# Input projections of two quarters at a time through DRAM, with S5 in batches of two groups beside them

## The chip, the core and the metric

One core of a Trainium2 chip runs the kernel. Its engines have instruction queues of their own: TensorE (PE) multiplies matrices, VectorE (DVE), ScalarE (ACT) and GpSimd (POOL) work on tiles, and SyncE (SP) issues transfers. What counts is the device time of one execution in microseconds; the median of several runs is compared.

## What is computed

One layer of a decoder is applied to 2048 new tokens of one sequence and, with stored states, to one further token of each of 8 samples. The width is 1024. Two mixers run on the same projections: S5, a diagonal state space with 32 groups of 64 complex states, and a gated delta net of 4 heads of 128 channels in chunks. Their outputs are joined and projected, and a feed-forward part with a short causal convolution follows:

```
def layer(x, ...):
    n = rmsnorm(x, norm1_g)
    proj = n @ w_in                                   # 512 of S5 | q, k, v | z | beta, a
    y_s5, s5_re, s5_im = s5_mixer(u_s5, ...)          # scan over time, gelu, gate w_glu
    y_gdn, gdn_s, gdn_buf = gdn_mixer(qkv, z, ...)    # conv of 4, silu, delta rule in chunks, norm, gate z
    x = x + jnp.concatenate([y_s5, y_gdn], axis=-1) @ w_out
    y_ffn, ffn_buf = conv_ffn(rmsnorm(x, norm2_g), ffn_buf, ffn_w_up, ffn_conv_w, ffn_w_down)
    return x + y_ffn, ...
```

All values are fp32. The outputs are the tokens, normed once more, and the mixers' and convolutions' last states.

## The kernel before

The tokens are cut into four quarters of 512 (`QT`); quarter 0 carries the 8 samples behind its tokens (520 columns). Activations lie transposed, channels on partitions. A product in fp32 is made of three products of float32r parts: every operand is split into a high part (`hi`, a copy on ACT) and an exact rest (`lo`, a subtraction on DVE; some on POOL), and `mm3` (lines 286 to 289) adds hi x hi, hi x lo and lo x hi. A projection of 128 output channels (`proj`, `mm24`) is thus 24 matmuls: 8 k tiles by three lines, L287 to L289. Its weights are loaded by `wcols` (L303) into a tile `wr` and split by `wsplit` through `split` (L71 on ACT, L72 on DVE or POOL). Each quarter of each use splits its weights anew; the eight tiles `W` and two tiles `wr` are rings that all of them share.

The stages, in the order of emission:

- Norm 1 of the quarters 3, 2, 1, 0 (`norm_first`), the S5 tables (`s5_setup`, to DRAM), and the S5 input projection of all quarters (`s5_in`, four weight tiles kept), whose result `u` goes to DRAM with time as (position in a chunk of 8, chunk).
- S5 proper: eight batches of four groups over all tokens (`s5_batch`), mixed with the heads of quarter 0 by the string `MIXERS`. A batch's first part (`b`) has the input product (L636), a rotation (L638 to L642) and 64-step scans in chains over four quarters (L649); its second part (`h`) has the rotation back (L656, L657), three output products (L665 to L668) and a gelu, and stores `y` to DRAM. Two of the wide multiplies (L641, L656) are POOL's.
- A head of a quarter has three parts: `F`, `gdn_front` (four projections for k, q, v, z from the quarter's normed tokens `nT`, the short convolution L820 to L824, norms, decay products), `I`, `gdn_inverse` (a triangular inverse by 31 steps L906, L907 and merges), `B`, `gdn_back` (the chunk recurrence, L953 to L966, output norm, gate, a store to `mixT` in DRAM).
- The output gate of S5 (`s5_glu`), and per quarter the output projection with residual (`ffn_out`, L1144), norm 2, the FFN's 22 steps of two channel tiles with up and down products (`ffn`, `ffn_down`, L1097), the final norm.

The string `FFN` puts the heads of quarters 1 to 3 beside the FFN of the quarter before: `r` is the next piece of the gate, output projection or FFN, `N` norms the next quarter again from stored x (`norm_again`, L276 to L283) and makes its columns (`gdn_cols`), `S` is the samples' delta step (`gdn_sample`), `G` stores final states. A scheduler then orders each engine's instructions from emission order, priorities and estimated times; engines execute their queue in that order, and a tile's ring of buffers decides when the next load may start.

## Time and profile before

| what | value |
|---|---|
| median of 3 runs | 2872.86 us (2869.67 to 2876.55) |
| span of the profiled execution, its own time here | 2874.3 us |
| PE busy | 2715.0 us, 94% |
| DVE busy | 2176.9 us, 76% |
| ACT busy | 1476.0 us, 51% |
| POOL busy | 609.6 us, 21% |
| DMA | 329.30 MB, mean 115 GB/s |
| mean granted TensorE clock | 0.964 of full speed |

The span runs from the first to the last instruction of one profiled execution. Busy shares are averages over stages that have different limits; the windows further down cut the span at the stages' ends. [...] Matmuls overlap in their records, so that a matmul's own duration is longer than the distance to the next one's start.

### The profile page before, as it was taken

The page shows a single profiled execution, that of the slowest core. Times are in us where ns is not written, and L with a number is a line of the kernel's source. Part 1 is how long each engine was busy: PE and PEld are TensorE (multiplying, and loading weights), DVE is VectorE, ACT ScalarE, POOL GpSimd, SP SyncE. Part 2 cuts the span into 40 slices and gives each one's busy share as a digit, 9 for nine tenths or more (in the row PEclk, how much of TensorE's full clock was granted, in tenths as well). Part 3 has the DMA queues.
Part 4 walks back from the last instruction along what each step waited for, and adds up shares of the span by engine and source line. Part 5 has one row for each costly group of instructions (what it writes and reads, how often), then busy time and mean ns, then how long its engine had stood idle before and what let it go on. Part 6 is the DMA issues. An engine that isn't in the chain of part 4 may idle for free.

```text
span 2874.3 us, 45554 instructions
## 1 busy us (share of the span) xinstructions
PE 2715.0 (94%) x16103; PEld 2337.9 (81%) x16103; DVE 2176.9 (76%) x4964; ACT 1476.0 (51%) x3051; POOL 609.6 (21%) x970
## 2 busy tenths in 40 slices
PE   6998788899999999998899999999999998999998
PEld 4798676786888999998887888878888787888887
DVE  8949898856688787778588687887768667676666
ACT  4446565653665554455564554555545445444444
POOL 4325332100121122222221100113211112211112
PEclk9999887898999999999999999999999999999999
DMA  7644433453644232233533333245333334523332
GB/s 205 199 134 132 113 109 92 105 133 104 182 110 117 77 103 87 89 97 111 155 115 109 100 91 98 84 137 174 93 96 97 90 93 144 157 88 96 95 97 74
DMA packets 457657, 329.30 MB, mean 115 GB/s; under 512 B 74960, under 2 KB 412249, under 8 KB 457412
## 3 DMA queue, kind: packets, MB, share of 16 engines
q1 hardware_dynamic: 447091, 297.77, 35.8%
q0 software_dynamic: 10336, 28.61, 3.4%
q8 instruction: 127, 2.08, 0.3%
q14 instruction: 103, 0.84, 0.1%
HBM read 279.29 MB, written 47.29 MB: 114 GB/s over the span
## 4 chain that ended last, share of the span: by engine, by line
PE 66%; DVE 17%; DMA 8%; ACT 4%; issue 3%; POOL 0%; SPq 0%; DVEq 0%; POOLq 0%; ACTq 0%
PE psmm L287 15%; PE psmm L288 15%; PE psmm L289 15%; PE psd L287 5%; PE psd L288 5%; PE psd L289 5%; DVE wlo L72 3%; DVE t L823 1%; ACT whi L71 1%; DVE X L907 1%; DMA xr<-xTD 1%; DMA mr<-mixT 1%; DVE x L1097 1%; DVE hh L649 1%; DMA wr<-in_w_out_dram 1%
## 5 line engine op out<-in xcount | busy, mean ns | idle before, releaser
L287 PE MATMUL psmm<-nT,whi 128*128 128x512 f32 (+2 forms) x3232 | 1115.5, 347 | 45.2 <-ACT whi L71 9.6
L288 PE MATMUL psmm<-nT,whi 128*128 128x512 f32 (+2 forms) x3232 | 1110.3, 344 | 4.8 <-DVE nT L224 3.0
L289 PE MATMUL psmm<-nT,wlo 128*128 128x512 f32 (+2 forms) x3232 | 1107.2, 343 | 1.7 <-POOL wlo L72 1.0
L287 PEld LDWEIGHTS psmm<-nT,whi 128*128 128x128 f32 x3232 | 622.5, 193 | 120.3 <-ACT whi L71 11.7
L288 PEld LDWEIGHTS psmm<-nT,whi 128*128 128x128 f32 x3232 | 624.5, 193 | 73.1 <-DVE nT L224 4.5
L71 ACT ACTIVATE whi<-wr 128x1024 fp32r<-128x1024 f32 x404 | 427.2, 1059 | 496.3 <-PE psmm L288 309.9
L289 PEld LDWEIGHTS psmm<-nT,wlo 128*128 128x128 f32 x3232 | 623.0, 193 | 72.4 <-issue 1.9
L72 DVE TENSOR_TENSOR wlo<-wr,whi 128x1024 fp32r<-128x1024 f32 x388 | 482.3, 1246 | 193.2 <-ACT whi L71 187.4
L1097 DVE TENSOR_TENSOR x<-psd,x 128x512 f32<-128x512 f32 (+2 forms) x464 | 255.6, 558 | 127.3 <-PE psd L289 125.2
L287 PE MATMUL psd<-gt,whi 128*128 128x512 f32 (+2 forms) x928 | 323.6, 350 | 12.7 <-DVE x L1097 10.4
L288 PE MATMUL psd<-gt,whi 128*128 128x512 f32 (+2 forms) x928 | 316.5, 342 | 0.0
L289 PE MATMUL psd<-gt,wlo 128*128 128x512 f32 (+2 forms) x928 | 314.6, 340 | 0.0
L1254 DVE SCALAR_TENSOR_TENSOR t<-raw,cc,t 128x512 f32<-128x512 f32 x352 | 271.5, 772 | 37.1 <-ACT t L1251 27.5
L1255 POOL COPY halo<-raw 128x2 f32<-128x2 f32 x176 | 49.6, 282 | 850.7 <-DVE raw L1250 765.9
L1251 ACT ACTIVATE t<-raw,cc 128x512 f32<-128x512 f32 (+1 forms) x176 | 127.2, 723 | 170.0 <-DVE raw L1250 156.7
L287 PEld LDWEIGHTS psd<-gt,whi 128*128 128x128 f32 x928 | 175.0, 189 | 42.5 <-DVE x L1097 18.8
L72 POOL TENSOR_TENSOR gt<-s,gt 128x512 fp32r<-128x512 f32 (+1 forms) x88 | 134.7, 1531 | 350.4 <-ACT gt L71 341.6
L288 PEld LDWEIGHTS psd<-gt,whi 128*128 128x128 f32 x928 | 175.1, 189 | 20.6
L289 PEld LDWEIGHTS psd<-gt,wlo 128*128 128x128 f32 x928 | 174.9, 189 | 20.8
L1107 POOL TENSOR_TENSOR sq<-sq 128x256 f32<-128x256 f32 (+1 forms) x112 | 109.8, 981 | 219.1 <-ACT sq L1105 213.1
L906 DVE TENSOR_TENSOR tm<-X,N 128x124 f32<-128x124 f32 (+30 forms) x496 | 125.4, 253 | 26.7 <-DMA N<-nD 17.6
L907 DVE TENSOR_TENSOR X<-X,tm 128x124 f32<-128x124 f32 (+30 forms) x496 | 129.6, 261 | 8.4
(503 smaller groups left out, 3666.5 us busy)
## 6 DMA issues: line engine op xcount, KB each, us to landing
wr<-in_ffn_w_up_dram SPq DMA_DIRECT2D x176, 512.0 KB
wr<-in_ffn_w_down_dram SPq DMA_DIRECT2D x88, 512.0 KB
wr<-in_w_in_dram SPq DMA_DIRECT2D x64, 512.0 KB
wr<-in_w_out_dram SPq DMA_DIRECT2D x64, 512.0 KB
xTD<-xT SPq DMA_DIRECT2D x32, 256.0 KB
N<-nD SPq DMA_DIRECT2D x16, 512.0 KB
mr<-mixT SPq DMA_DIRECT2D x32, 256.0 KB
xr<-xTD SPq DMA_DIRECT2D x32, 256.0 KB
```

Source lines behind the costliest of these rows:

```text
L71: nc.scalar.activation(hi, raw, AF.Copy)
L72: (eng or nc.vector).tensor_tensor(lo, raw, f32(hi), op=OP.subtract)
L287: nc.tensor.matmul(out, lhsT=wh, rhs=xh, start=first, stop=False)
L288: nc.tensor.matmul(out, lhsT=wh, rhs=xl, start=False, stop=False)
L289: nc.tensor.matmul(out, lhsT=wl, rhs=xh, start=False, stop=last)
L906: nc.vector.tensor_tensor(m, X[:, :, j:j + 1].to_broadcast(sh), N[:, j:j + 1, j + 1:].to_broadcast(sh), op=OP.mult)
L907: nc.vector.tensor_tensor(X[:, :, j + 1:], X[:, :, j + 1:], m, op=OP.add)
L1097: nc.vector.tensor_tensor(x2[:, j, b0:b1], p, x2[:, j, b0:b1], op=OP.add)
L1107: c.nc.gpsimd.tensor_tensor(acc[0], acc[0], s, op=OP.add)
L1251: nc.scalar.activation(t[:, :n], raw[:, 2:2 + n], AF.Copy, scale=w[2])
L1254: nc.vector.scalar_tensor_tensor(t[:, :QT], raw[:, j:j + QT], w[j], t[:, :QT], op0=OP.mult, op1=OP.add)
L1255: nc.gpsimd.tensor_copy(c.halo[:, ch], raw[:, QT:QT + 2])
```

## The change

All input projections leave the heads. A generator `in_pass` takes two quarters: it loads and splits the four S5 weight tiles and makes `u` of both quarters; then, four column tiles of one head at a time (k, q, v, z), it projects both quarters with one load and split of the weights, evicts PSUM to a tile `rw` (ACT, or DVE with the row scales in quarter 1), and stores it to `rawD` in DRAM. It runs first for quarters 1 and 0 (string `PASS1`, with three heads' parts of quarter 0), then for 3 and 2 (string `PASS2`, with S5's batches, the columns, the samples' step and the last head of quarter 0). S5's rest is in `MIXERS` behind it, then come the FFN's pieces: nine for the gate and quarter 0's output projection without a head, then three lines of sixteen pieces with four heads each, then quarter 3's FFN. `gdn_front` loads q, k, v (with three halo columns) and z of its quarter from `rawD` through SP instead of projecting them. S5 runs in 16 batches of two groups; its two multiplies on POOL go to DVE. All lo parts of weights are DVE's now (16 of 404 were POOL's), and there are 376 instead of 404. `norm_again` falls away, and the S5 rotation tables are made in two passes of 16 groups, not four of 8.

```diff
-UNQ = (3, 2, 1)
+UNQ = (1,)
-WQ = lambda nc: nc.gpsimd
+WP = 3000
-PRE = "uuuuucuulu"
-MIXERS = "bFIbhbFhhbIbBhbhFBbFIhhbBhx"
-FFN = "IBNFrrIrFrrrrSrrBFrIIBrrrFIrBBrNFrIFrrrrBIrrFrrBIrrrrBFrrrrINBrFIrFrrBFIrrrrIrBrBrrrrrrrFrrrrrIBrrrGrrrrrrrrrrrrrrrrrrrr"
+PASS1 = "ppppppppFppppppppIFppppppppBIFpppppppp32BI"
+PASS2 = "cFSbBbIphBpbphppbphppbphppbphppbphppbphppbphpppbphpppbphppbphppb"
+MIXERS = "hbhbhbhhhhhhhhx"
+FFN = ("rrrrrrrrr"
+       "rrFrrIrBFrrIrBFrrIrBFrrIrBrr"
...
+       "G")
...
+def in_pass(c, qs, nTs, rsBs):
...
+    ws = [wcols(c, c.w_in, t * 128) for t in range(4)]
+    for q in qs:
+        for t in range(4):
+            s5_in(q, t, ws[t])
+    yield
+    for h in range(4):
+        ts = [t + h for t in (4, 0, 8, 12)]
+        with c.tc.high_priority(WP):
+            ws = [wcols(c, c.w_in, 512 + ti * 128) for ti in ts]
+        for q in qs:
+            for ti, w in zip(ts, ws):
+                n = ncols(q)
+                raw = c.V("rw")
+                for b0, b1, p in projw(c, q, nTs[q], w):
+                    evict(raw[:, b0:b1], q, p, b0, b1)
+                nc.sync.dma_start(c.rawD[ti, :, q * QT:(q + 1) * QT], raw[:, :QT])
...
+                yield
...
-    """4 groups (64 channels) over all prompt tokens, and their samples"""
-    gs = slice(4 * t, 4 * t + 4)
+    gs = slice(2 * t, 2 * t + 2)
...
-    nc.gpsimd.tensor_tensor(Xw[:, :, :, 0:64], Xw[:, :, :, 0:64], St[:, :, None, 1:65].to_broadcast(sh(64)), op=OP.mult)
+    tt(Xw, Xw, St[:, :, None, 1:65].to_broadcast(sh), op=OP.mult)
...
-    nc.gpsimd.tensor_tensor(hw, H, St[:, :, None, 0:64].to_broadcast(sh(64)), op=OP.mult)
+    tt(hw, H, St[:, :, None, 0:64].to_broadcast(sh), op=OP.mult)
...
-def gdn_front(c, q, h, nT, col, hp):
+def gdn_front(c, q, h, col, hp):
...
+    def load(dst, ti):
+        if q:
+            nc.sync.dma_start(dst[:, 0:QT + 3], c.rawD[ti, :, q * QT - 3:(q + 1) * QT])
...
-        pr = proj(c, q, nT, c.w_in, 512 + ti * 128)
...
-        for b0, b1, p in pr:
-            nc.scalar.activation(raw[:, 3 + b0:3 + b1], p, AF.Copy)
-            nc.scalar.activation(t[:, b0:b1], p, AF.Copy, scale=w[3])
+        load(raw, ti)
+        nc.scalar.activation(t[:, :n], raw[:, 3:3 + n], AF.Copy, scale=w[3])
```

What stands in the engines' queues now, at three places. First PE in the S5 stage. `pss` are S5's products, `psmm` projections, `psi` and `psb` pieces of a head. Before:

```order
L636 MATMUL pss<-U,Fm 128x256 x2
L928 MATMUL psi<-T2T_145,Z 32x32 x4
L636 MATMUL pss<-U,Fm 128x256 x2
L289 MATMUL psmm<-nT,wlo 128x264
L938 MATMUL psi<-TT,LT 64x64 x4
L636 MATMUL pss<-U,Fm 128x256 x2
L941 MATMUL psi<-T2T_145,Z_2865 64x64 x4
L636 MATMUL pss<-U,Fm 128x256 x2
L959 MATMUL psb<-rv,T2T_145 128x128
L665 MATMUL pss<-U,Tm 128x256
L963 MATMUL psb<-vn,kg 128x128
L964 MATMUL psb<-vn,AT 128x128
```

After, in the second pass:

```order
L274 MATMUL psmm<-nT,whi 128x512
L275 MATMUL psmm<-nT,whi 128x512
L276 MATMUL psmm<-nT,wlo 128x512
L274 MATMUL psmm<-nT,whi 128x512
L275 MATMUL psmm<-nT,whi 128x512
L276 MATMUL psmm<-nT,wlo 128x512
L674 MATMUL pss<-U,Tm 128x256
L685 MATMUL pss<-Us,Fm 128x8 x2
L689 MATMUL pss<-Us,Tm 16x8
L690 MATMUL pss<-h_4674,Em 16x8
L676 MATMUL pss<-hh,Em 128x256
L677 MATMUL pss<-hw,Es 128x256
```

The S5 products and head pieces that followed one another with single projection matmuls between them now stand behind whole projections over 512 columns (L274 to L276 are L287 to L289 of before).

Second, PE in the new order where the second pass ends:

```order
L276 MATMUL psmm<-nT,wlo 128x512
L674 MATMUL pss<-U,Tm 128x256
L685 MATMUL pss<-Us,Fm 128x8 x2
L689 MATMUL pss<-Us,Tm 16x8
L690 MATMUL pss<-h_4674,Em 16x8
L689 MATMUL pss<-Us,Tm 16x8
L676 MATMUL pss<-hh,Em 128x256
L677 MATMUL pss<-hw,Es 128x256
L674 MATMUL pss<-U,Tm 128x256
L676 MATMUL pss<-hh,Em 128x256
L677 MATMUL pss<-hw,Es 128x256
L690 MATMUL pss<-h_4674,Em 16x8
```

Up to there projections alternate with S5; from there on only S5's small products stand in the queue, until the gate's first products. Before, no such place exists, since projections of heads run on through the FFN.

Third, DVE where quarter 0's FFN hands over to quarter 1's output projection (`x` from `psmm` and `xr` is the residual sum that evicts a product, `wlo` a split, L823 and L841 the convolution of a head's front). Before:

```order
L195 SCALAR_TENSOR_TENSOR nrm<-x_6015,cc,rq 128x256
L72 TENSOR_TENSOR wlo<-wr,whi 128x1024
L72 TENSOR_TENSOR nT_6016<-nrm,nT_6016 128x256
L1144 TENSOR_TENSOR x_6015<-psmm,xr 128x256 x2
L957 SCALAR_TENSOR_TENSOR rv<-psb,col,vt 128x128
L195 SCALAR_TENSOR_TENSOR nrm<-x_6015,cc,rq 128x256 x2
L72 TENSOR_TENSOR wlo<-wr,whi 128x1024
L72 TENSOR_TENSOR nT_6016<-nrm,nT_6016 128x256 x2
L961 TENSOR_SCALAR vn<-psb,hc 128x128
L72 TENSOR_TENSOR wlo<-wr,whi 128x1024
L823 SCALAR_TENSOR_TENSOR t<-raw,cc,t 128x512 x3
```

After:

```order
L1163 TENSOR_TENSOR x_7807<-psmm,xr 128x256 x3
L71 TENSOR_TENSOR wlo<-wr,whi 128x1024
L1163 TENSOR_TENSOR x_7807<-psmm,xr 128x256
L71 TENSOR_TENSOR wlo<-wr,whi 128x1024 x2
L841 SCALAR_TENSOR_TENSOR t<-raw,cc,t 128x512 x2
L71 TENSOR_TENSOR wlo<-wr,whi 128x1024
L841 SCALAR_TENSOR_TENSOR t<-raw,cc,t 128x512
L852 TENSOR_TENSOR kq<-s,t 128x512
L841 SCALAR_TENSOR_TENSOR t<-raw,cc,t 128x512 x3
L852 TENSOR_TENSOR kq<-s,t 128x512
L841 SCALAR_TENSOR_TENSOR t<-raw,cc,t 128x512 x3
L96 TENSOR_SCALAR rkq_a<-ssq,epscol 128x8
```

Between two evictions of the output projection there now stands a whole head's convolution; before, it came behind evictions, norm (L195) and recurrence (L957, L961).

## Rows read from the trace of the kernel before

**Rows 1.** The page: busy time by engine, and the chain that ended last.
```profile
PE 2715.0 (94%) x16103; PEld 2337.9 (81%) x16103; DVE 2176.9 (76%) x4964; ACT 1476.0 (51%) x3051; POOL 609.6 (21%) x970
...
PE 66%; DVE 17%; DMA 8%; ACT 4%; issue 3%; POOL 0%; SPq 0%; DVEq 0%; POOLq 0%; ACTq 0%
```

**Rows 2.** Timeline of PE, 2640 us: start, duration, engine, line, operation.
```profile
2640.10 0.39 PE L288 MATMUL psmm<-nT,whi 128*128 128x512 f32 x1
...
2641.02 0.39 PE L289 MATMUL psmm<-nT,wlo 128*128 128x512 f32 x1
```

**Rows 3.** Timeline of PE, 2500 us, over 256 columns.
```profile
2500.01 0.28 PE L287 MATMUL psmm<-nT,whi 128*128 128x256 f32 x1
...
2500.84 0.28 PE L288 MATMUL psmm<-nT,whi 128*128 128x256 f32 x1
```

**Rows 4.** Windows by stage: length, busy us of each engine, PEclk, DMA share, GB/s.
```profile
0.00:150.00 150.00, 118.78 (x613) 96.32 (x613) 127.12 (x465) 69.29 (x159) 52.76 (x72) 0.94 0.68 200
150.00:200.00 50.00, 48.01 (x387) 45.22 (x387) 21.30 (x62) 18.47 (x45) 11.48 (x8) 0.93 0.42 122
200.00:525.00 325.00, 271.64 (x1711) 234.95 (x1710) 282.89 (x797) 188.71 (x503) 115.35 (x137) 0.86 0.41 113
525.00:881.00 356.00, 336.42 (x2071) 287.50 (x2072) 252.79 (x699) 189.09 (x453) 50.50 (x75) 0.92 0.47 128
881.00:1337.00 456.00, 448.59 (x3505) 426.04 (x3503) 362.29 (x861) 232.96 (x463) 97.60 (x189) 1.00 0.34 97
1337.00:1488.00 151.00, 138.80 (x968) 127.59 (x967) 107.15 (x228) 87.88 (x193) 42.14 (x55) 0.97 0.45 132
...
2522.00:2846.00 324.00, 323.68 (x1395) 261.41 (x1394) 219.71 (x296) 145.79 (x216) 47.12 (x98) 1.00 0.30 91
2846.00:2875.00 29.00, 19.39 (x138) 16.22 (x136) 17.68 (x46) 12.44 (x28) 14.77 (x22) 0.92 0.20 75
```

**Rows 5.** Windows of 75 us inside the S5 stage, same columns.
```profile
225.00:300.00 75.00, 64.32 (x418) 59.46 (x417) 73.04 (x173) 48.84 (x128) 40.37 (x40) 0.91 0.41 112
300.00:375.00 75.00, 55.16 (x344) 47.04 (x342) 60.19 (x188) 33.09 (x79) 22.22 (x23) 0.77 0.35 97
```

**Rows 6.** DVE groups by shape: out<-in, count, busy us, mean ns, idle before.
```profile
L72 DVE TENSOR_TENSOR wlo<-wr,whi 128x1024 fp32r<-128x1024 f32 x388 | 482.3, 1246 | 193.2 <-ACT whi L71 187.4 <-DMA out_dram<-S0s 1.8 <-PE psd L287 0.9
...
L823 DVE SCALAR_TENSOR_TENSOR t<-raw,cc,t 128x512 f32<-128x512 f32 x144 | 112.2, 779 | 11.9 <-ACT t L820 10.5 <-ACT sta L790 0.2
...
L649 DVE TENSOR_TENSOR_SCAN hh<-rho,hh 128x64 f32<-128x64 f32 x128 | 43.1, 394 | 0.1
...
L72 DVE TENSOR_TENSOR nT<-nrm,nT 128x512 fp32r<-128x512 f32 x32 | 25.1, 790 | 0.4 <-ACT nT L71 0.3
...
L957 DVE SCALAR_TENSOR_TENSOR rv<-psb,col,vt 128x128 f32<-128x128 f32 x64 | 22.1, 345 | 10.0 <-PE psb L955 9.6
...
L195 DVE SCALAR_TENSOR_TENSOR nrm<-xT,cc,rsB 128x512 f32<-128x512 f32 x24 | 20.7, 860 | 4.7 <-DMA xT<-xTD 4.6
...
L966 DVE TENSOR_TENSOR ot<-psb,ot 128x128 f32<-128x128 f32 x64 | 18.0, 281 | 0.0
...
L642 DVE TENSOR_TENSOR hh<-hh,Xw 128x1024 f32<-128x1024 f32 x8 | 9.7, 1215 | 0.0
```

**Rows 7.** POOL groups by shape.
```profile
L641 POOL TENSOR_TENSOR Xw<-Xw,tab 128x1024 f32<-128x1024 f32 x8 | 19.3, 2408 | 27.0 <-ACT Xw L640 23.6 <-PE psmm L289 3.3
```

**Rows 8.** The chain of waits up to 560 us: start, duration, transfer.
```profile
57.31 2.83 DMA uD<-up
...
461.85 2.81 DMA xT<-xTD
```

**Rows 9.** PE groups by shape, 0 to 881 us.
```profile
L846 PE MATMUL psf<-ident,kq 128*128 128x128 f32 x64 | 11.4, 312 | 1.5 <-DVE kq L833 1.5
...
L954 PE MATMUL psb<-Sst,kq 128*128 128x128 f32 x51 | 12.8, 337 | 7.6 <-DVE ot L966 6.6 <-DVE zs L980 1.0
```

**Rows 10.** The page's groups: the inverse's steps on DVE.
```profile
L907 DVE TENSOR_TENSOR X<-X,tm 128x124 f32<-128x124 f32 (+30 forms) x496 | 129.6, 261 | 8.4
```

326 lines of the change are left out of this document (159 added, 167 removed).

## Prediction

> **What bounds the kernel now.** I read the busy shares and the chain of waits first: TensorE (PE) is busy 94% of a span of 2874.3 us and carries 66% of the chain, VectorE (DVE) 76% and 17% [rows 1]. So time is PE's work at full pace plus what PE loses. The pace is in the timeline: a product over 512 columns starts every 0.23 us [rows 2], one over 256 every 0.118 us [rows 3]; 24 of the former (three lines by eight k tiles) are one projection of a quarter, 5.57 us. Counting every matmul of the program at these paces gives 2585 us of PE work; the span loses 289.
>
> The windows by stage [rows 4] say where. In the front, up to 881 us (the first product of a quarter's FFN), I count 672 us of work, so 209 lost; after it 1913 in 1993, so 80 lost, nearly all where one quarter's FFN hands over to the next (1337 to 1488 is such a stretch) and at the end. The worst stage is S5 beside the first heads, 200 to 525: PE work 218 of 325 us. There DVE is busy 87% of the time, and the granted clock is 0.86; in its stretches DVE stands at 73 of 75 us, then the clock at 0.77 [rows 5]. DVE is the limit there, and PE, short of work, is granted less clock between the gaps. From 881 on PE has its clock at 1.00 and DVE has room: 362 of 456 us.
>
> The change keeps the amount of both engines' work (the same matmuls; DVE's total by my count within 1%) and moves it: projections and S5 into one another, the heads of three quarters beside the FFN. It is a question of where DVE's load falls.
>
> **The change part by part.**
> The sizes that change are small. Sixteen lo parts go from POOL to DVE and 28 splits fall away (projection weights now serve two quarters): DVE 388 - 376 = 12 of 1.246 us less [rows 6]. S5's batches of two groups double the small rotations, at 0.2 to 0.3 us of DVE each, and halve the wide operations. The two multiplies that leave POOL (8 each of 2.4 us [rows 7]) cost DVE 16 x 1.2 = 19 us [rows 6].
>
> *Front.* I went through the new order on PE and DVE, matmuls at [rows 2, 3], DVE operations at their rows, overlapped as before (durations sum to 2445 us for 2177 busy, factor 0.89).
> - Up to the first pass of projections: PE work 92, but the second norm waits for DVE, which also has the S5 tables (91 to 112 us of it); before, 150 us hold 127 of DVE [rows 4]. I take 151: loss 59, some 20 more than before.
> - First pass: 32 projections of two quarters, 178 us, with 30 of head pieces; DVE has some 123. PE is dense, no wait but an eviction: loss 7, to 366.
> - Norms of the other two quarters and their S5 inputs: work 70, loss 18, to 454. The norm's chain (transpose, scales, split) feeds every product.
> - Columns, the last head of quarter 0, the samples' step: work 46. The step borrows the weights' tiles, so the next pass's weights wait behind it (ACT's split, then PE's products). The trace has no such order; bounds are 10 (the split alone) and 60 (its whole extent, some 85 us before, beside other work). I take 35, to 535.
> - Second pass with twelve S5 batches: work 204, DVE some 110. This is what the change buys: S5's scans (128 of 0.39 us [rows 6]) and the 19 us of multiplies lie behind products over 512 columns; without that cover they would stand on the path as they do now. Loss 10, to 749.
> - The rest of S5: the projections are used up, and four more first parts and six second ones follow with DVE 48 us against PE 22. Then y goes through DRAM (stores and reloads take 2.8 us each [rows 8]). Work 22, loss 38 (28 for DVE, 10 for the handover), to 809.
> - Gate, mixing, output projection and norm of quarter 0: work 172. Before, heads of the next quarter filled it; the new order has none there. Each step waits for the one before it through DRAM or DVE. Before, this stretch, from 525 to 881 [rows 4], lost 46 with heads as filling, and the samples' step was in it. Bounds 20 and 60; I take 45, to 1026.
>
> The front thus loses 59 + 7 + 18 + 35 + 10 + 38 + 45 = 212, as much as now: what S5 no longer costs is lost at the stages that have become bare.
>
> *FFN.* At 1026 us PE has 1770 left (1913, less 178 for eight heads' projections, 8 x 4 x 5.57, and some 12 for two quarters' columns, which now come earlier, plus some 45 for heads which now come later: before, eight fronts and 6.4 backs, at 8 products of L846 and L954 a head [rows 9], now four of each). DVE has 2177 - 684 = 1493 left in the kernel of before (684 is the sum of the first four windows [rows 4]). It loses 32 splits of projection weights (36 us, 1.246 us each [rows 6], with the factor) and the norms of two quarters (16 x (0.86 + 0.79) x 0.89 = 24 [rows 6]; the split's 0.79 is a like row of nT); it gains four fronts with inverses at about 27 us each (nine L823 [rows 6], 31 pairs of L907 and its like [rows 10], three of the seven 128-column groups of 64, 18 to 22 us each [rows 6], whose first and last stand there) and 2.4 backs at 6, that is 122. So 1555. The last quarter has no heads, as before: 237 us of DVE in its 343 us of products [rows 4]. That leaves about 1315 of DVE beside 1428 of PE in three quarters: DVE at 0.92 of PE's work. Before, I count 0.86, 0.84 and 0.74, and inside a quarter that was met with PE at 98 to 100%, as from 881 to 1337 [rows 4]. At the boundaries it was not: 1337 to 1488 has PE busy 139 of 151 [rows 4], and I put its loss at 24, with the next two at 11 and 21. In the new order the heads are spread evenly, so the out projection's evictions and the norm share DVE with a head's front: 152 and 148 us of DVE against 120 of PE at the first two boundaries. I take 33 for each of them, 18 for the third (the last quarter follows, without heads), 3 x 8 inside the quarters, 10 at the end: 118, where 80 is lost now.
>
> *Reloads.* Each head loads q, k, v, z from DRAM on SP's queue. SP only issues transfers, in order: behind a raw store that waits for its eviction, or a reload, stand the next weights' loads, for which ACT's split and then PE wait. If they are issued early, nothing waits: I cost them at 0. Bounds: 0, and four waits of 2.8 us [rows 8] in each of twelve heads, 134. In the queue's order a head's four reloads stand among the weight loads of the pieces before its front, so I stay at the lower end.
> [...]
>
> Sum: 2585 + 212 + 118 = 2915 us, 1.4% over the profiled execution, whose span lies 0.05% above the median 2872.86; so I leave the sum uncorrected.
>
> **The rivals.**
> *Other side, faster: the dense projections hold PE's clock, and the bare stages come cheap.* Place: 366 to 1026. Before, the clock below 1.00 over the first 881 us [rows 4] comes to 0.06 x 150 + 0.07 x 50 + 0.14 x 325 + 0.08 x 356 = 87 us. If samples, S5's rest and gate cost 20, 15 and 25 (not 35, 38, 45), and norms and start 10 less each, the front loses 212 - 78 = 134, and the time is 2837. It decides by when the first FFN product runs: with my 118 behind it, at 986 us the kernel ties with before; earlier, it wins. For it: PE has its full clock wherever it is dense. Against it: the long chains remain, and nothing stands between their links.
> [...]
> *DVE becomes the bound of three quarters.* The S5 stage ran DVE at 87% as its limit [rows 4]. At 87%, 1315 us take 1511 against PE's 1428, a loss of 83, near mine without the end (108). At 82%, 1604: loss 176, and the time 2915 + 68 = 2983. For it: splits (1.25 us) and head pieces queue in one order, and PE waits for both. Against: DVE reached 97% for 75 us [rows 5].
> *The change doesn't do what it says: the round trip serializes.* Weight loads stand behind raw stores and reloads on SP, whose waits hold the queue; a quarter of the 134 showing gives 2915 + 34 = 2949.
> A tie comes when front and FFN lose 289 together, between the forecast and the fast rival.
>
> **How the numbers follow.** The forecast as worked out has 0.48 (0.03 of it within 0.2% of now), the fast rival 0.29 (0.03 in the tie), DVE's bound 0.14, the queue 0.09. A difference under 0.2% is about what measurements of this kernel can't tell from none. So faster 0.26, same 0.06, slower 0.68. The range takes in the fast rival's 2837 and DVE's 2983 with some 7 us more, leaving out about a tenth on each side: 2830 to 2990. The likeliest case alone spans 2875 to 2965 (front 185 to 245, FFN 105 to 135).
>
> **What would show it.** In the windows of the changed kernel: both passes with PE near 100% at clock 1.00 and S5's scans inside the second; the first FFN product near 1026; a stretch after the last projection in which PE is below two thirds and DVE above 80%; DVE at 0.85 or more through three quarters, and boundaries with PE waiting for DVE's x (the residual's sum) or wlo. Wrong would be: first FFN product before 986 (the fast rival); PE's waits in the FFN ending on DVE inside the quarters, not at their ends (DVE's bound); ACT or DVE waiting for the raw tiles' DMA (the queue).

## The result, and where the time went

The changed kernel takes 3135.66 us (median of 4 runs, 3131.25 to 3141.51), before 2871.7 us in the same comparison: a ratio of 1.0912, 95% interval 1.0893 to 1.093. Forecast were 2915 us, 2830 to 2990. The direction was right, the size was not: 9% and not 1.4%.

The page of the changed kernel: busy time by engine, and the chain that ended last (compare [rows 1]).

```profile
PE 2788.0 (89%) x16103; PEld 2376.5 (76%) x16103; DVE 2139.9 (68%) x5001; ACT 1460.9 (47%) x3058; POOL 504.6 (16%) x866
...
PE 69%; DVE 13%; DMA 8%; ACT 5%; issue 3%; SPq 1%; POOL 0%; ACTq 0%; DVEq 0%; POOLq 0%
```

No engine has become fuller. PE fell from 94% to 89%, DVE from 76% to 68%; in the chain DVE's share fell from 17% to 13%, and PE, ACT and SP's queue took it. The windows are cut at the same events as [rows 4] (length, then busy us of PE, PEld, DVE, ACT, POOL, then PEclk, DMA share, GB/s; PEclk is the granted TensorE clock as a share of full speed):

```profile
0.00:180.00 180.00, 125.02 (x679) 107.23 (x679) 118.32 (x399) 55.45 (x136) 59.42 (x68) 0.76 0.50 148
180.00:424.00 244.00, 224.60 (x1459) 199.90 (x1458) 124.18 (x379) 86.22 (x221) 9.89 (x42) 0.93 0.34 100
424.00:507.00 83.00, 74.01 (x384) 56.98 (x385) 37.16 (x109) 40.87 (x108) 6.42 (x9) 0.94 0.54 159
507.00:611.00 104.00, 74.59 (x290) 50.54 (x289) 69.77 (x269) 34.82 (x107) 10.77 (x22) 0.70 0.32 85
611.00:826.00 215.00, 215.00 (x1035) 172.54 (x1034) 98.48 (x273) 86.12 (x204) 11.94 (x20) 1.00 0.43 129
826.00:903.00 77.00, 47.98 (x167) 33.31 (x165) 44.63 (x148) 32.16 (x92) 7.20 (x13) 0.61 0.28 82
903.00:1142.00 239.00, 192.23 (x1176) 171.09 (x1176) 128.81 (x253) 113.54 (x212) 28.43 (x38) 0.88 0.46 126
1142.00:1563.00 421.00, 403.31 (x3280) 391.48 (x3279) 334.05 (x789) 215.51 (x443) 92.25 (x181) 0.96 0.31 91
1563.00:1718.00 155.00, 113.87 (x813) 106.49 (x812) 105.16 (x244) 75.96 (x152) 39.90 (x47) 0.87 0.45 130
1718.00:2104.00 386.00, 375.90 (x1859) 300.13 (x1858) 322.25 (x701) 212.72 (x431) 48.15 (x101) 0.99 0.33 98
2104.00:2265.00 161.00, 116.33 (x815) 108.34 (x814) 111.96 (x257) 76.43 (x164) 41.22 (x49) 0.83 0.42 124
2265.00:2650.00 385.00, 375.43 (x1854) 300.01 (x1853) 319.99 (x696) 211.07 (x431) 47.46 (x109) 0.99 0.33 99
2650.00:2774.00 124.00, 106.32 (x782) 100.49 (x782) 87.88 (x155) 61.78 (x122) 39.17 (x48) 0.90 0.47 142
2774.00:3099.00 325.00, 324.67 (x1401) 262.34 (x1399) 220.23 (x297) 145.82 (x216) 47.59 (x98) 1.00 0.30 91
```

In order: up to the first pass, first pass, norms, samples' step and last head of quarter 0, second pass, S5's rest, gate to the norm of quarter 0, then FFN quarters and, between them, the boundaries. An FFN quarter begins here with its first down product (1142 us); a boundary runs from the last few down products of one quarter (2104 us) to the first of the next (2265 us). The second pass (611 to 826) is what the change was made for: PE busy 215.00 of 215 us, clock 1.00, S5's work on DVE beside it. Around it lie the stretches at a clock of 0.70, 0.61 and 0.88, and three boundaries at 0.87, 0.83 and 0.90 (before's first has 0.97 [rows 4]). In none of these is DVE near full (45 of 77 us in S5's rest, 105 of 155 and 112 of 161 at the first two boundaries).

Loss, here and below, is the time of a marked matmul in the trace less the work ahead of it in PE's program, each product at the pace of [rows 2, 3]. Before and after by work done:

```
PE work done, us        92   300   370   416   620   642   815   2585 (end)
before, at             127   411   523   579   827   849  1028   2874
after, at              186   423   506   611   826   903  1142   3129
```

Up to 620 us of work the two are level: what the second pass wins is what start and samples' step lose. From there to the first down product of the FFN (815) the changed kernel loses 115 us more, and in the rest 141. By stage (to the last S5 product, gate to first down product, then quarters q and boundaries b, then q3 with the end), for the runs on which the argument rests (before and the runs made from it reach the last S5 product at 344 to 371 us of work, the others at 635 or 642):

```
                            S5  gate   q0  b1  q1  b2  q2  b3  end   time, us
before                     153    56   15  15   9   9   5  17   10   2871.7
after                      261    66   38  48  20  54  20  23   13   3135.7
heads off boundary         258    60   39  29  22  41  20  30   13   3099.6
heads as before            262   104   44  27  29  10  12  10   13   3098.5
heads one ahead            262    70   41  27  23  23  20  15   13   3081.0
before, even heads         166    90   12  51   6  49   6  24   11   3002.2
before, round trip         167   127   49  38  37  10  13  18   11   3056.6
reloads together           249    66   25  47  16  53  13  31   13   3101.2
one tap left out           260    67   37  50  14  53  15  25   13   3121.7
down lo on POOL            259    67   58  48  38  54  42  26   15   3194.7
S5 all in pass             218    68   48  48  23  57  17  24   13   3103.8
samples in gate            211    92   38  49  19  60  19  25   12   3111.6
all moves                  186    94   39  27  20  23  21  17   12   3026.0
moves that gained          181    92   34  27  25  18  17  19   12   3009.7
```

The times of the experiments are single runs; those of the changed kernel spread over 10 us, those of before over 13 (2866.3 to 2879.2). Differences of 10 to 20 us between single runs are therefore readings, not proofs. With these cuts before's boundaries lose 15, 9 and 17 us; the prediction, which cut them elsewhere, had 24, 11 and 21.

The stretch from the gate to quarter 0's norm is not bare to its end. The nine pieces without a head are eight of the gate and one of loads; the pieces of quarter 0's output projection are the first four of the string's next line, and the first head of quarter 1 starts among them.

### The profile page after: what moved, and what is told of

Same layout as the page of the kernel before. It is cut to its first block, busy times and chain, and to the rows that moved or that the text cites. A ratio compares the mean times of both kernels' runs of the same rounds, so it can differ in the third digit from the quotient of the medians.

```text
span 3129.5 us, 45763 instructions
## 1 busy us (share of the span) xinstructions
PE 2788.0 (89%) x16103; PEld 2376.5 (76%) x16103; DVE 2139.9 (68%) x5001; ACT 1460.9 (47%) x3058; POOL 504.6 (16%) x866
## 4 chain that ended last, share of the span: by engine, by line
PE 69%; DVE 13%; DMA 8%; ACT 5%; issue 3%; SPq 1%; POOL 0%; ACTq 0%; DVEq 0%; POOLq 0%
PE psmm L274 16%; PE psmm L275 15%; PE psmm L276 15%; PE psd L274 4%; PE psd L276 4%; PE psd L275 4%; DVE wlo L71 3%; DMA wr<-in_w_out_dram 2%; DMA raw<-rawD 2%; DVE t L841 2%; ACT whi L70 1%; DMA N<-nD 1%; DVE x L1195 1%; DMA mr<-mixT 1%; DVE x L1116 1%
## 5 line engine op out<-in xcount | busy, mean ns | idle before, releaser
L274 PE MATMUL psmm<-nT,whi 128*128 128x512 f32 (+2 forms) x3232 | 1117.8, 348 | 74.5 <-DVE x L1163 44.5
L276 PE MATMUL psmm<-nT,wlo 128*128 128x512 f32 (+2 forms) x3232 | 1108.2, 343 | 2.0 <-DVE wlo L71 2.0
L274 PEld LDWEIGHTS psmm<-nT,whi 128*128 128x128 f32 x3232 | 623.9, 194 | 154.6 <-DVE x L1163 45.7
L276 PEld LDWEIGHTS psmm<-nT,wlo 128*128 128x128 f32 x3232 | 624.3, 193 | 71.3 <-DVE wlo L71 3.1
L70 ACT ACTIVATE whi<-wr 128x1024 fp32r<-128x1024 f32 x376 | 397.3, 1059 | 504.0 <-PE psmm L275 344.3
L71 DVE TENSOR_TENSOR wlo<-wr,whi 128x1024 fp32r<-128x1024 f32 x376 | 467.2, 1246 | 195.9 <-ACT whi L70 173.3
L274 PE MATMUL psd<-gt,whi 128*128 128x512 f32 (+2 forms) x928 | 328.0, 355 | 18.8 <-DVE x L1116 13.0
L276 PE MATMUL psd<-gt,wlo 128*128 128x512 f32 (+2 forms) x928 | 317.7, 345 | 3.2 <-DVE wlo L71 3.1
L275 PE MATMUL psd<-gt,whi 128*128 128x512 f32 (+2 forms) x928 | 319.1, 345 | 1.4 <-POOL gt L71 1.4
L1273 DVE SCALAR_TENSOR_TENSOR t<-raw,cc,t 128x512 f32<-128x512 f32 x352 | 269.9, 768 | 26.0 <-ACT t L1270 19.6
L274 PEld LDWEIGHTS psd<-gt,whi 128*128 128x128 f32 x928 | 176.1, 190 | 48.5 <-DVE x L1116 21.1
L276 PEld LDWEIGHTS psd<-gt,wlo 128*128 128x128 f32 x928 | 175.9, 191 | 25.5 <-DVE wlo L71 4.9
L841 DVE SCALAR_TENSOR_TENSOR t<-raw,cc,t 128x512 f32<-128x512 f32 x144 | 113.7, 789 | 22.3 <-ACT t L839 20.1
```

The lines of the kernel that those rows point to most:

```text
L70: nc.scalar.activation(hi, raw, AF.Copy)
L71: (eng or nc.vector).tensor_tensor(lo, raw, f32(hi), op=OP.subtract)
L274: nc.tensor.matmul(out, lhsT=wh, rhs=xh, start=first, stop=False)
L275: nc.tensor.matmul(out, lhsT=wh, rhs=xl, start=False, stop=False)
L276: nc.tensor.matmul(out, lhsT=wl, rhs=xh, start=False, stop=last)
L841: nc.vector.scalar_tensor_tensor(t[:, :QT], raw[:, j:j + QT], w[j], t[:, :QT], op0=OP.mult, op1=OP.add)
```

## What a boundary waits for

Of after, the wait list of PE between the FFN of quarter 1 and that of quarter 2 (what waited, for what: us in total, times, longest):

```profile
PE psf L865 <- DVE kq L852: 14.6, 2, 9.0
PE psmm L274 <- DVE x L1163: 11.2, 2, 10.5
```

The first, the larger one, is the transposition of a head's k, q and v, at the end of a chain that begins with a reload (chain of waits: start, duration, what):

```profile
2177.68 4.16 DMA raw<-rawD
2181.92 0.73 ACT t L839
...
2187.03 0.70 DVE kq L852
2187.77 1.13 PE psf L865 x4
```

What stands behind the second, in the timeline (start, duration, engine, line, operation, idle time before and its releaser):

```profile
2204.70 1.75 SPq L916 DMA_DIRECT2D nD<-LT  x4
...
2207.63 0.53 SPq L918 DMA_DIRECT2D N<-nD  x1
...
2208.25 7.58 SPq L1148 DMA_DIRECT2D xr<-xTD  x2
...
2213.85 0.29 DVE L925 TENSOR_TENSOR tm<-X,N 128x124 f32<-128x124 f32 x1 [4.29 <-DMA N<-nD]
2214.17 0.29 DVE L926 TENSOR_TENSOR X<-X,tm 128x124 f32<-128x124 f32 x1
...
2214.69 0.75 DVE L1163 TENSOR_TENSOR x<-psmm,xr 128x256 f32<-128x256 f32 x2
...
2215.16 0.58 PE L274 MATMUL psmm<-nT,whi 128*128 128x256 f32 x1 [10.50 <-DVE x L1163]
```

A head's inverse has its turn in DVE's queue. Its input `N` was stored to DRAM and asked back at 2207.6; DVE stands idle 4.29 us for it. Behind it in the same queue is L1163, which evicts a product of the output projection that is done, and PE waits 10.50 us for that eviction. But DVE's queue alone does not explain the wait: L1163 also reads the residual `xr`, whose reload stands on SP behind the inverse's stores and its reload, and these behind a weight load that had held SP for 14.6 us:

```profile
SPq L290 <- DVE wlo L71: 14.6, 1, 14.6
```

The reload was issued at 2208.25 as soon as its turn came, and by the marks of its semaphore in the trace it landed at 2214.29, 0.4 us before the eviction. The same holds for the longest such wait at the boundary before (10.3 us; `xr` issued at 1661.9, landed at 1667.9, eviction at 1668.2) and in quarter 0's output projection (10.9 us; last part issued at 1083.8, landed at 1089.3, eviction at 1089.6). So in these places the end is set by SP's order, the weights and the head's transfers ahead of the residual's; DVE's order alone would have cost 0.3 or 0.4 us more. Neither PE nor DVE is full at this boundary (116 and 112 of 161 us); the order of the queues made a transfer's latency a wait of PE (10.50 us, with DVE's 4.29 for `N` inside it). The chain of waits of the same boundary (start, duration, what):

```profile
2121.91 0.95 PE psb L998 x4
2122.88 0.76 DVE zs L999
2123.66 2.23 DMA mixT<-zs
2125.91 4.37 DMA mr<-mixT
2130.30 0.64 ACT nT L70
2130.98 0.80 PE psmm L274 x2
```

The last head of quarter 2 ends (L998), is stored, and is reloaded for the mixing product, which goes on at 2131.0, 8 us after the head's end. In the string that head ends two pieces ahead of the mixing product; in the order of before it ends nine pieces ahead.

## Experiments on the order of the heads

**Heads off the boundary.** Each FFN line has four pieces of output projection and norm, then twelve of FFN.

```diff
-       "rrFrrIrBFrrIrBFrrIrBFrrIrBrr"
+       "rrrrFrIrBFrrIrBFrIrBFrrIrBrr"
```

> The changed kernel (3135.7 us) with the order of emission of the FFN alone changed: in each of the three lines no head's part stands among the four pieces of the output projection and norm; the four heads stand closer together in the twelve pieces behind. Theory A, chains in the queues: at the boundaries neither PE nor DVE is full (2100 to 2250: PE busy 105, DVE 101 of 150 us), because a head's front and inverse (reload, convolution, transposes, another reload) stand in the in-order queues among the products of the output projection. Then the two boundaries lose 25 to 35 us less each, the first one some 10: 3045 to 3085 us. Theory B, DVE's throughput: the heads' DVE work now lies in fewer pieces that were near DVE's limit (126 of 150 us), and what the boundary wins the quarter loses: 3115 to 3150 us.

3099.6 us, 36 less, between the two theories: boundaries 48 + 54 lose 29 + 41, the third 30 where it lost 23, and the quarters lose what they lost (39, 22, 20), although the same heads stand in fewer pieces. So the boundaries' loss is not DVE's throughput alone; but only a part of it goes with the place.

**Heads as before.** The FFN's string is that of before, without N, S and the parts of quarter 0.

> The changed kernel with the FFN's string of before (without its norms, the samples and the two parts of quarter 0 that the change does earlier): the same twelve heads, but begun in the gate's pieces and done nine to eleven pieces ahead of the product that mixes them, where the changed kernel ends them two pieces ahead. Theory D, lead: what the boundaries lose (48, 54 and 23 us, after 15, 9 and 17 before) is that each quarter's output projection waits for its own last head's store and reload, with the next quarter's first head in the same queues; with before's lead these losses fall to 60 in sum, the quarters' own 38, 20 and 20 to 30, and the gate is filled: 3000 to 3050 us. Theory E, filling: in before the projections of heads stood in these places as PE work, and what is now there is DVE work; then the boundaries stay at 100 or more and the gate gains at most 15: 3080 to 3130 us.

3098.5 us: boundaries 27, 10 and 10, near before's, so their loss was the order of the heads. The gate pays: 104, where it lost 66, and the first two quarters lose 44 and 29 for 38 and 20, so that the time as a whole is in theory E's range. Heads put there bring chains and, without projections, few products; that this is why the gate pays was not tested by itself.

**Even heads in before.** The other way round, the changed kernel's string in the kernel before (the edit is written shorter here than in the kernel).

```diff
-FFN = "IBNFrrIrFrrrrSrrBFrIIBrrrFIrBBrNFrIFrrrrB...
+FFN = "IBrrrrSrrrrr" + 3 * ("N" + "rrFrrIrBFrrIrBFrrIrBFrrIrBrr") + "G..."
```

> The kernel before with the changed kernel's even FFN string (nine pieces without a head, then three lines with four heads each, the norm of the next quarter ahead of each line); projections stay with their heads. Theory D, lead: the boundaries lose as in the changed kernel, 40 to 60 more in sum for the two, and the gate stands bare: 2960 to 3020 us. Theory E, filling: the projections fill the boundaries (each is 5.6 us of PE work) and little is lost there, the gate alone costs some 20: 2885 to 2930 us.

3002.2 us, 4.4% more than before with an order of letters: boundaries 51, 49 and 24, close to the changed kernel's, though here the heads bring their projections along. Filling (theory E) is not enough, and order costs here too. That the figures agree is partly chance: this string also puts `N`, the next quarter's norm, at the head of each line, where before has it nine or ten pieces earlier and the changed kernel not at all, and its reloads stand on this boundary's chain:

```profile
1936.59 3.26 DMA xT<-xTD
...
1949.73 4.37 DMA xT<-xTD
```

No run parts `N` from the heads here. The quarters lose 12, 6 and 6: the changed kernel's 38, 20 and 20 are not the heads' order alone.

**Heads one ahead.** Off the boundary, and the first head of quarter 1 in the gate, so that each quarter's last head ends five pieces ahead of its mixing product, not two.

```diff
-FFN = ("rrrrrrrrr"
+FFN = ("rrrrrFrIrrBr"
...
-       "rrFrrIrBFrrIrBFrrIrBFrrIrBrr"
+       "rrrrFrIrBFrrIrBFrIrBFrrIrBrr"
...
+       "rrrrFrIrBFrrIrBFrrIrBrrrr"
```

> The changed kernel with the FFN's string of the run with all moves and nothing else: the heads off the pieces of the output projection, and one head ahead (the first of quarter 1 in the gate). Against the run that only takes the heads off these pieces (3099.6 us, boundaries 29, 41 and 30 lost), theory D says that the lead of a head is worth 10 to 20 us at each boundary, less what the gate pays for its head: 3060 to 3085 us. If the lead is worth nothing, 3095 to 3110 us.

3081.0 us, as theory D said: boundaries 27, 23 and 15 against 29, 41 and 30 with the place alone, for 10 more in the gate. In time the place is worth 36 us and the lead 19 more, in single runs.

## Experiments inside the quarters

**Reloads by POOL.**

```diff
-            nc.sync.dma_start(dst[:, 0:QT + 3], c.rawD[ti, :, q * QT - 3:(q + 1) * QT])
+            nc.gpsimd.dma_start(dst[:, 0:QT + 3], c.rawD[ti, :, q * QT - 3:(q + 1) * QT])
...
```

> The changed kernel with the heads' reloads of q, k, v and z issued by POOL instead of SP, so that they don't stand in SP's queue behind weight loads that wait for their buffers, nor weight loads behind them. Theory C, SP's queue: the round trip is what costs; 30 to 70 us come back: 3065 to 3105 us, and the convolution's wait for the reload (20 us in sum) nearly goes. Theories A and B: the reloads were not what stood in the way, 3120 to 3150 us.

3153.9 us, 18 more, above both ranges. ACT's wait for the reload, which theory C wanted nearly gone, falls from 19.7 to 16.7 us only:

```profile
ACT t L839 <- DMA raw<-rawD: 16.7, 14, 3.4
```

By this run SP's queue is not what holds these reloads, and theory C in this form falls. It says nothing of the residual's reload above, which stayed on SP, and what issuing from POOL costs by itself was not shown.

**Round trip alone, in before.** A head's projections are evicted to a tile, stored and loaded again at once.

```diff
+        rw = c.V("rw")
+        for b0, b1, p in pr:
+            nc.scalar.activation(rw[:, b0:b1], p, AF.Copy)
+        nc.sync.dma_start(c.rawD[ti, :, q * QT:(q + 1) * QT], rw[:, :QT])
...
+        nc.sync.dma_start(dst[:, :QT], c.rawD[ti, :, q * QT:(q + 1) * QT])
```

> The kernel before with the round trip alone: each head's four projections stay where they are, but are evicted to a tile, stored to DRAM and loaded again ahead of the convolution. It adds 64 stores and 64 loads of 256 KB to SP's queue and about 6 us to each product's way in a head. If the round trip is a main cost of the change, 2930 us or more; if the heads' lead hides it, 2865 to 2895 us.

3056.6 us, 190 more; I had 2895 as the most if lead hid it. The waits of ACT and PE in this kernel:

```profile
ACT t L831 <- DMA raw<-rawD: 136.0, 43, 7.1
...
PE psmm L287 <- ACT rw L818: 53.6, 22, 9.8
```

43 times ACT stands at the convolution's first product until the reload lands, 136 us in all, and behind it in ACT's queue are the evictions that PE waits for (53.6 us) and the weights' `whi`. This store lies right ahead of its reload, so the figure is no price for the changed kernel, whose stores are hundreds of us old for quarters 1 to 3; there the same wait is 19.7 us:

```profile
ACT t L839 <- DMA raw<-rawD: 19.7, 18, 2.6
```

But it shows a way in which a reload hurts here: at the engine that uses it (136.0 us of ACT) and at what is queued there (53.6 us of PE).

**One tap left out.** One of two multiply-adds of the FFN's convolution isn't computed.

```diff
-                for j in (1, 0):
+                for j in (1,):
```

> The changed kernel with one of the two multiply-adds of the FFN's short convolution left out (176 of 0.77 us on DVE; the oldest tap is not computed, so this part of the result is another). DVE loses some 30 us in each quarter and nothing is added to any other engine. Theory B, DVE's share holds PE back inside the quarters: of the 38, 20 and 20 us lost there half or more comes back, and the boundaries stay (48, 54, 23): 3080 to 3105 us. If waits of a head's chains or reloads hold PE, the quarters stay as they are: 3120 to 3140 us.

3121.7 us; DVE busy in quarter 1 falls from 322 to 295 us, and the loss there from 20 to 14, in quarter 2 from 20 to 15, in quarter 0 hardly (37 for 38). DVE's share is a part, some 12 of 78 us by this one run, not the half that theory B wanted.

**Reloads together.** In quarter 1 of the changed kernel the reloads stand on the chain of waits, at 4.0 to 5.4 us each, where the prediction had priced one at 2.8:

```profile
1824.00 4.76 DMA raw<-rawD
...
1838.62 4.02 DMA raw<-rawD
...
1938.92 5.36 DMA raw<-rawD
```

In this run q, k and v are asked for at the front's start, each into its own tile.

```diff
+    raws = [c.V("raw") for _ in range(3)]
+    for raw, ti in zip(raws, (4 + h, h, 8 + h)):
+        load(raw, ti)
...
```

> The changed kernel with the three reloads of q, k and v issued together at the start of a head's front, each into its own tile, instead of one ahead of each convolution. Theory C3, the reloads' latency inside the quarters: on the chain of waits of one quarter (1730 to 2090 us) the reload of a raw tile stands with 3.9% of 360 us, 14 us, of 20 lost; the second and third reload now land beside the first convolution, so 5 to 10 us come back in each of three quarters and some at the boundaries: 3095 to 3120 us. If ACT's and PE's order around the head is what waits, not the reload, the quarters keep their 38, 20 and 20: 3125 to 3145 us.

3101.2 us: quarters 25, 16 and 13, which is 24 of 78 back, and 12 in the front, where quarter 0's heads reload too; the third boundary loses 8 more. The latency of reloads is the larger known part of the quarters' loss, by one run. By the waits alone (19.7 us on ACT in all, 16.9 here) one would not have seen it. I take it that the time shows up as later evictions and splits and as a lower clock; shown is the clock, 0.96 in the 421 us that hold quarter 0 above, 0.99 in as many from that quarter's start here:

```profile
1130.00:1551.00 421.00, 405.39 (x3370) 395.34 (x3370) 343.39 (x805) 219.19 (x453) 97.16 (x185) 0.99 0.33 96
```

Some 25 us of the quarters' excess over before (54 now lost against 29) stay unexplained.

**Lo parts of w_down on POOL**, in the changed kernel and in before.

```diff
-    return wsplit(c, lambda wr: c.nc.sync.dma_start(wr, w[r0:r0 + 128, :]))
+    return wsplit(c, lambda wr: c.nc.sync.dma_start(wr, w[r0:r0 + 128, :]), c.nc.gpsimd)
```

> The changed kernel with the lo parts of the down projection's weights (88 of 376) made by POOL, 2.4 us each, instead of DVE, 1.25 us: DVE loses 98 us of busy time in the FFN, some 27 in each quarter, POOL (504 us busy) gets 214. Theory B for what is left inside the quarters (38, 20 and 20 us lost, against 15, 9 and 5 before): DVE at 83% busy holds back PE; then 10 or more of each quarter come back, 3085 to 3110 us. Theory C2, waits of another kind (reloads, chains of a head): no gain, and POOL's slower parts may cost, 3125 to 3160 us.

> The same edit in the kernel before, whose quarters have DVE at 79, 80 and 72% and lose 15, 9 and 5 us: by either theory at most 15 us come back, 2855 to 2885 us. A gain as large as in the changed kernel would mean that the even heads and the missing projections are not what makes DVE short there.

3194.7 us, and 2905.0 in before: 59 and 28 more, above every range that I had given. The quarters lose 58, 38 and 42. As a test of DVE's share it failed, because it did not relieve DVE: in quarter 1 (1737 to 2141 us here) DVE is busy 334 us, where it was 322, with twenty-one splits fewer. Some of its other operations grew, which the last section comes back to.

## Experiments on the front

**All S5 in the pass.** All sixteen first and fifteen second parts stand in the second pass (the new string is written shorter here than in the kernel).

```diff
-PASS2 = "cFSbBbIphBpbphppbphppbphpp...bphpppbphpppbphppbphppb"
-MIXERS = "hbhbhbhhhhhhhhx"
+PASS2 = "cFSbBbIphB" + "pbph" * 14 + "ppp"
+MIXERS = "hhx"
```

> The changed kernel with all sixteen first parts and fifteen second parts of the S5 batches inside the second pass of projections (there were thirteen and eleven), so that the stretch of S5 behind the last projection (826 to 900 us, PE work 22) is one second part and the samples. If that stretch costs what its DVE work without projections costs, some 30 to 40 us come back, and the pass, with DVE at half, takes the batches for nothing: 3095 to 3110 us. If the chain of scans and the store and reload of y set the end of S5 whatever stands beside it, 3125 to 3145 us.

3103.8 us, 32 less. The last projection now ends at 851 us and S5's last product at 861, so that the stretch behind the projections takes 10 us instead of 77, and the pass 244 (from the same product as before, here at 607) instead of 215:

```profile
607.00:851.00 244.00, 240.34 (x1176) 192.18 (x1174) 139.66 (x410) 111.47 (x284) 17.42 (x30) 1.00 0.45 134
851.00:861.00 10.00, 4.47 (x26) 3.16 (x25) 5.33 (x12) 5.13 (x12) 2.08 (x4) 0.95 0.49 137
```

The pass takes three more first and four more second parts with PE at 240 of 244 us and the clock at 1.00. Under projections these parts cost PE little more than their own work, as the change meant; its string left part of them outside. What they cost outside is not DVE's busy time, as the prediction had it, but a chain: in that stretch of the changed kernel DVE is busy 45 of 77 us, the clock is 0.61, and the longest of PE's waits in sum are for the matrix of a batch's first product:

```profile
PE pss L647 <- DMA Fm<-FD: 10.5, 3, 4.5
```

**Samples in the gate.**

```diff
-PASS2 = "cFSbBbIph...
+PASS2 = "cFbBbIph...
-FFN = ("rrrrrrrrr"
+FFN = ("rrSrrrrrrr"
```

> The changed kernel with the samples' delta step moved from the start of the second pass into the pieces of the gate, where before has it too. If the weights of the second pass wait for the tiles that the step borrows, the stretch from 507 to 611 us (work 46, loss 58) loses 30 to 45 less, and the gate, which is bare, takes the step for 0 to 15: 3095 to 3125 us. If the loss there is the last head of quarter 0 and the columns, a chain of its own, nothing is gained: 3130 to 3155 us.

3111.6 us, 24 less: the first head projection of the second pass starts at 514 us instead of 588, the loss up to the last S5 product falls from 261 to 211, the gate's rises from 66 to 92, more than the 15 that I had allowed. The step's tiles did hold up the pass's weights; in the changed kernel ACT's split waits for the step's product:

```profile
ACT whi L70 <- PE psf L1067: 16.6, 3, 8.4
```

Half of the gain is paid in the gate.

**S5 inputs before the second norm.** The S5 projection of the first quarter is emitted before the norm of the other.

```diff
+            st.ps = in_pass(c, (1, 0), nTs, rsB)
+            next(st.ps)
             smp = norm_samples(c, pre)
             norm(0, xs)
-            st.ps = in_pass(c, (1, 0), nTs, rsB)
             next(st.ps)
...
```

> The changed kernel with the S5 input projection of quarter 1 (and of 3 in the second pass) emitted ahead of the norm of the other quarter. Up to the first pass the changed kernel loses some 88 us where before loses about 39 in its first 150; if that is because PE has no product to do while the second quarter's norm waits for x and DVE, 25 to 45 come back: 3090 to 3110 us. If the loads of x and the constants set the start for any order, 3125 to 3140 us.

3143.6 us: no gain. These products already ran at 22 to 40 us, as soon as their operands were there; the scheduler had drawn them forward.

**Tables behind the first eight projections.**

```diff
             next(st.ps)
+            emit("pppppppp")
             s5_setup(c)
...
```

> The changed kernel with the S5 tables, the columns and the samples' halos emitted behind the first eight projections of the first pass instead of ahead of it; nothing but the order differs. Up to 180 us the changed kernel does 92 us of PE work, and from 40 to 112 us PE has little but the tables' small products, DVE being busy 46 of 50 us with the tables while the second norm waits for it. If the tables on DVE are what delays the first pass, 25 to 45 us come back: 3090 to 3110 us, with DVE's tables under the first projections. If the second quarter's x or its scales set the pace, or the tables only move to another bare place, 3125 to 3140 us.

3148.8 us, no gain, and 8 us above my second range. The first pass starts earlier (92 us of work are done at 170, not 186) and takes longer (300 at 432, not 423): the tables are chains of small products and DVE steps, and stand in both queues wherever they are. The start stays as it is; what sets it is open.

**S5 by two groups in before**, with both multiplies on DVE.

```diff
-MIXERS = "bFIbhbFhhbIbBhbhFBbFIhhbBhx"
+MIXERS = "bbFIbbhhbbFhhhhbbIbbBhhbbhhFBbbFIhhhhbbBhhx"
...
```

> The kernel before with S5 alone changed: sixteen batches of two groups (two in the place of one, rings twice as deep in half as large tiles), both POOL multiplies on DVE. If the small batches themselves cost (twice the rotations, 19 us of multiplies on a DVE that is the limit from 200 to 525 us), 2890 to 2920 us, all of it in that stretch; if they cost nothing there, 2865 to 2880 us.

2895.3 us, 18 more than the run of before beside it: 10 to the last S5 product, 8 in the gate. Beside the first heads, where DVE is busy 87% of the time [rows 4], small batches cost; the second pass, which has them under projections, loses 11 us in all.

**All moves**, and **the moves that gained** (without the tables' place, with the reloads together; no edit but those above).

```diff
-FFN = ("rrrrrrrrr"
+FFN = ("rrSrrrFrIrrBr"
...
```

> The changed kernel with the moves of this study together: tables behind the first eight projections, all S5 first parts inside the second pass, the samples' step in the gate, and the heads one ahead (the first head of quarter 1 in the gate, none in the pieces of an output projection). By the losses won alone or expected (32, 24, 35 for the three, 60 to 80 for the heads' order), if they add: 2960 to 2990 us. If they eat one another, DVE being the limit of what they fill, 3010 to 3050 us. Either way it stays above before, since what the front bares and what DVE costs inside the quarters is not touched.

> The changed kernel with every move that gained by itself: S5 inside the second pass, the samples in the gate, heads off the output projection's pieces and one ahead, the three reloads together; the tables in their old place. From the run with all moves (3026 us): 10 to 25 us back for the tables, 25 to 35 for the reloads, so 2970 to 2995 us if they add. If they fill the same gaps, 3000 to 3025 us. Below 2900 us would say that most of the change's price was order alone.

3026.0 and 3009.7 us: 110 and 126 less than the changed kernel; the gains found one by one come to some 145 (32, 24, 55, 34). They add for the most part, but both times lie in the ranges that I had given for moves that fill the same gaps. Some 135 us over before remain: 28 by the last S5 product, 36 more in the gate, and in the FFN the quarters (34, 25, 17 against 15, 9, 5) and boundaries (27, 18, 19 against 15, 9, 17). I found no version that beats before.

## Why the prediction failed, by its own steps

The frame held: PE's work of 2585 us is the same, and the time is that plus losses, 544 instead of the 330 summed. The terms:

```
                         start pass1 norms samples pass2 S5 rest gate | quarters b1 b2 b3 end
forecast                    59     7    18      35    10      38   45 |       24 33 33 18  10
measured                    94    29    13      59    11      55   66 |       78 48 54 23  13
```

- *The second pass and S5 under it: right; the first pass: too small.* The second pass lost 11 for 10 forecast, and more of S5 fits (all S5 in the pass). The first pass lost 29 for 7: clock 0.93, with waits for quarter 0's heads and for evictions; no run parts these.
- *The bare stages: right in place, each 45 to 70% larger than forecast, the mechanism right in part.* Samples' step 59 for 35, near its upper bound of 60; S5's rest 55 for 38; gate 66 for 45, above its bound of 60; the start 94 for 59. Where I had bounds I had taken values near their middle. PE does what it has to do there at a clock of 0.61 to 0.88 in the windows above. The samples' step was what I said it was, tiles that hold up weights. S5's rest was not: 28 of its 38 us were DVE's, and the sign that I named, DVE above 80%, failed with 58% (45 of 77 us). That DVE is the limit of S5 was read from [rows 4, 5], where the window with the lowest clock, 0.77, has DVE at 60 of 75 us. The gate was not bare either: a head of quarter 1 stands in quarter 0's output projection, with a boundary's wait of 10.9 us.
- *The boundaries: the sign was right, the reason was not.* I took DVE's 152 and 148 us against PE's 120 and wrote 33. The measured 48 and 54 come with DVE at 105 of 155 and 112 of 161. What decides is lead and place of the heads: before's order in the changed kernel costs 27 and 10, and place and lead alone bring 48 and 54 down to 27 and 23 (heads one ahead). The even order in the kernel before costs 51 and 49, a part of which can be `N`'s. The order of the third place that I showed ahead of the prediction had it: a whole head's convolution between two evictions. I costed its busy time, not what it waits for, nor the residual's reload, which stands behind its transfers on SP, nor that the last head ends two pieces ahead of its use.
- *Inside the quarters: the step that failed most.* "That was met with PE at 98 to 100%" was carried over from a kernel without reloads; 8 a quarter, where 38, 20 and 20 were lost. A smaller part is DVE (12 of 78), a larger one the reloads (24), each by one run; some 25 of the excess over before stay open.
- *Reloads at nothing: wrong.* They were costed at SP, and off SP the kernel is no faster (reloads by POOL). They cost where they are used: they stand on the chain of quarter 1 with 4.0 to 5.4 us each, ACT waits for them (19.7 us in all), and asking for three at once gave 34 us back. That reloads issued early cost nothing, as the forecast had it, no run shows.
- *The rivals.* The fast one fell at its mark: the first FFN product came at 1142, not before 986. The full clock that it counted on held in the second pass (1.00, PE busy 215 of 215 us) and not in the first (0.93, PE busy 225 of 244 us). DVE as the bound of three quarters named the right stretch and, for the most part, the wrong reason: DVE is at 0.79 to 0.83 there, and with 27 us of its work taken out of a quarter the quarters gave back 12 of 78. The queue rival put the wait at SP behind weight loads; for the heads' reloads the runs found it at ACT, and at SP, behind a weight load and a head's transfers, for the residual's reload at the boundaries, where it is partly right. The range was too narrow because every loss that I bounded had its upper end in a case of its own, while they came all at once: with the upper bounds of samples and gate (60 each) and DVE's rival in the FFN (68) the sum is 3023. Of the last 106 us, 74 are start, first pass and S5's rest (35, 22 and 17 over), to which I had given no upper end, and 30 are FFN beyond DVE's rival: reloads and the heads' lead, as far as the runs tell.

## What to carry to other kernels

Compare queues, not only engine sums: where a moved stage has DRAM reloads in its chain, ask for each engine what is queued behind the instruction that waits for the reload, and how far ahead of its use the last producer ends. Order can cost more than any engine's sums show: another order of letters, with the same instructions, made the kernel before 4.4% slower. A stage that lost its filling cost its chain here: S5's rest took 77 us at a clock of 0.61, and 10 us with all S5 in the pass, which grew by 29 us at a clock of 1.00. So what is moved out of a stage should be costed at the stage it leaves, at the upper bound.

## What was not expected of the hardware

POOL's subtractions held up DVE's multiplies and multiply-adds that read two tiles. DVE groups in the changed kernel (count, busy us, mean ns of one):

```profile
L1273 DVE SCALAR_TENSOR_TENSOR t<-raw,cc,t 128x512 f32<-128x512 f32 x352 | 269.9, 768 | 26.0 <-ACT t L1270 19.6 <-POOL raw L1271 2.1 <-POOL gt L71 1.3
...
L1269 DVE TENSOR_TENSOR raw<-psmm,rs 128x256 f32<-128x256 f32 x126 | 52.7, 418 | 3.2 <-ACT raw L1268 3.0
...
L1282 DVE TENSOR_TENSOR s<-s,t 128x512 f32<-128x512 f32 x66 | 45.3, 687 | 3.4 <-ACT s L78 2.6
```

and the same with 88 lo parts of 128x1024 on POOL:

```profile
L1273 DVE SCALAR_TENSOR_TENSOR t<-raw,cc,t 128x512 f32<-128x512 f32 x352 | 318.8, 906 | 52.3 <-ACT t L1270 45.5
...
L1282 DVE TENSOR_TENSOR s<-s,t 128x512 f32<-128x512 f32 x66 | 75.4, 1142 | 9.7 <-ACT s L78 8.7
...
L1269 DVE TENSOR_TENSOR raw<-psmm,rs 128x256 f32<-128x256 f32 x126 | 52.5, 417 | 7.9 <-ACT raw L1268 7.7
```

The mean multiply of two tiles went from 687 to 1142 ns, the mean multiply-add from 768 to 906; the eviction, which reads one operand from PSUM, stayed at 418 and 417. In before the same edit gave 1149, 934 and 417. The means hide what happens to a single operation:

```profile
1738.25 2.50 POOL L71 TENSOR_TENSOR wlo<-wr,whi 128x1024 fp32r<-128x1024 f32 x1 [0.93 <-ACT whi L70]
1738.46 2.84 DVE L1282 TENSOR_TENSOR s<-s,t 128x512 f32<-128x512 f32 x1
```

The multiply starts under POOL's subtraction and ends 0.55 us after it. Of the 58 operations of L1273, L1282 and L1283 over 512 columns that start under such a subtraction, 54 end 0.55 to 0.56 us after it, however early they started, and take up to 2.9 us; those that meet no work of POOL take 686 (the multiplies) and 746 ns (the multiply-adds) on average. In before it is 57 of 60. The 14 evictions that start under one take 410 to 434 ns. In the changed kernel, whose weights' lo parts are DVE's, the 15 multiply-adds of L1273 and L841 over 512 columns that start under a subtraction of POOL's for the down products (`gt`) all end 0.54 to 0.55 us after it and take 1.17 to 1.79 us, against 747 ns on average where they meet no work of POOL. So such an operation was, with few exceptions (4 of 58, 3 of 60), not slowed by a share: it did not end until POOL's had. Moving lo parts to POOL to relieve DVE thus cost DVE most of what it took away: here 88 x 1.25 = 110 us were taken, and the two groups shown alone grew by 49 and 30.
